# Two projections as separate runs with a stored partial sum, in a single-core hybrid layer

## The chip, the cores and the metric

The kernel runs on one core of a Trainium2 chip. A core has a matrix engine (TensorE, PE in the profile; its weight loads are the row PEld), a vector engine (DVE), a scalar engine (ACT), a general engine (POOL) and a queue engine (SP) that issues most transfers. PE writes to PSUM, eight banks of 128 x 512 floats; DVE and ACT read them from there. The metric is the device time of one execution in microseconds, the median of several runs.

## The reference, cut to what matters

One layer works on 2048 latent tokens of width 1024. One input projection feeds two token mixers, branch A (a gated DeltaNet, four heads of 128) and branch B (windowed attention, eight heads of 64). Each branch is gated, projected to width 1024 by a matrix of its own, scaled by a sigmoid gate computed from the input, and the two are summed:

```
def _merge(ya, yb, ga, gb, w_proj_a, w_proj_b, w_out):
    y = jax.nn.sigmoid(ga) * (ya @ w_proj_a) + jax.nn.sigmoid(gb) * (yb @ w_proj_b)
    return y @ w_out
...
    x = x + gate[:, None] * _merge(ya, yb, ga, gb, w_proj_a, w_proj_b, w_out)
```

The change concerns the two products with w_proj_a and w_proj_b, their scaling and their sum.

## The kernel before, in words

All values are float32. A product is made of three matmuls on rounded parts: each operand is split into a high part and a low part, and high x high, high x low and low x high are summed in one PSUM bank. The 2048 tokens are worked on in four groups of 512 (0 to 3).

The order is: modulation and normalisation; the input projections with the short convolutions; the triangular inverses of branch A beside the gate projections of groups 2 and 3; the scan of branch A beside gates of groups 1 and 0; attention; the branch projections (`project`); the output product (with seven products for each pair of 256-token units instead of eight). Intermediate tensors go to DRAM and come back: `yasp` and `ybsp` hold the two gated branches, `gasp` and `gbsp` the gates (as tanh values), `ysp` the merged result, one tensor for each group.

A planner orders each engine's instructions ahead of time. Work traced earlier has the higher priority, and later work fills in where the planner's own clock sees an engine free. Engines then run their lists in order. Only the output stage has its order on DVE, ACT, POOL and PE written out by hand.

Attention takes query blocks of 128 tokens in the order of groups 1, 2, 0, 3, and each block in two units (one for each key-value head), 32 units in all. A unit's scores are computed two units ahead. While attention runs it holds seven PSUM banks, and everything else on PE shares one bank (tag `acc`). Two kinds of other work fill PE there. First come the gate tiles that the scan has left over: `gates` (L841) runs column tiles 15 to 23, each for group 1 and then for group 0, 24 matmuls a tile. Then comes `project` (L1234) for groups 1, 2 and 0. Group 3 needs attention's last units and runs behind it, with all eight banks.

`project` makes eight tiles of 128 output columns for a group. A tile has two halves of 12 matmuls (L1247 to L1249), the first with branch A and w_proj_a, the second with branch B and w_proj_b, and each half has a bank of its own. DVE scales each half by its gate (L1258: gate plus one, times PSUM), with the gate loaded into tile `ta` or `tb`; POOL (DVE for group 3) adds them (L1263), and the sum is stored into `ysp`. `ta` uses two buffers with the tag `rt`, `tb` two of a pool of its own. `paced(i)` (L877) keeps the matmuls of a half behind the last matmul of attention's unit i: tiles of group 1 behind units 7 to 14, of group 2 behind 15 to 22, of group 0 behind 23 to 30.

`load_y` (L1216) loads the two branches of a group in pieces of 256 KB through the two staging buffers tagged `wr`, and splits them (ACT rounds, L1227; DVE subtracts, L1228). Branch A's parts lie in buffers that the gate weights used (`wh`, `wl`), branch B's in buffers of their own. `proj_w` (L1202) loads w_proj_a and w_proj_b through the same staging buffers, in two column halves, each with both matrices. Their tiles take the place of the input of groups 0 (w_proj_a) and 1 (w_proj_b), so each waits for the last gate that reads that group.

For group 3, tiles 6 and 7 keep both halves in PSUM. `late_sum` (L1267) scales and adds them in the output stage, at places in its hand-written order on DVE, ahead of splits that its products wait for.

## Time and profile before

| what | value |
|---|---|
| time, median of 3 runs | 1997.59 us (1997.26 to 2005.6) |
| profiled execution, its own time | 1992.9 us |
| its span, first to last instruction | 1991.2 us |
| mean granted TensorE clock | 0.989 of full speed |
| PE busy | 1917.4 us, 96% of the span |
| DVE, ACT, POOL busy | 1502.1, 802.6 and 692.1 us |
| bytes moved by DMA | 333.12 MB, mean 167 GB/s |
| projections' matmuls (L1247 to L1249) | 256 of each, the first starting at 1464.7 us |

Times in the trace are counted from the first instruction. A row of the timeline reads: start, duration, engine, line, operation, what it writes and reads, its shape, and in brackets how long the engine had stood idle before it and what ended that. A matmul's end is modelled, and the next one starts before it, so durations of PE overlap. A row whose engine has a q behind its name is an issue by that engine's sequencer, most often of a transfer.

### The profile page before, as it was taken

Reading aid. Unit: us, or ns where it says so; the run is one execution under the profiler, and the core shown is the slowest. Engines: PE = TensorE matmul, PEld = TensorE weight load, DVE = VectorE, ACT = ScalarE, POOL = GpSimd, SP = SyncE. Lnnn points to the kernel's source line nnn. Section 1 sums busy time; section 2 is a strip of 40 time slices with the busy share of each in tenths; the row PEclk is TensorE's granted clock in tenths of the full one; section 3 lists DMA queues with packets and bytes.
Section 4 is the critical chain, followed back from the end, with each engine's and each line's share of the span. In section 5 each row is a group of like instructions: output and inputs, shape, how many; then the busy total and the mean of one; then the engine's idle time right before and its main releaser. Section 6 shows DMA issues by size and latency. Waiting matters only on the chain. (4 is left out here: it accounts for less than half of the span.)

```text
span 1991.2 us, 32088 instructions
## 1 busy us (share of the span) xinstructions
PE 1917.4 (96%) x10947; PEld 1605.6 (81%) x10947; DVE 1502.1 (75%) x2869; ACT 802.6 (40%) x1994; POOL 692.1 (35%) x768
## 2 busy tenths in 40 slices
PE   7999999989999999999999999999989999999998
PEld 4888888779998787877888888788778887877786
DVE  6979766668776999999677776536686878747888
ACT  5755545554443323111222233225665656532221
POOL 2742211235542202004222234323555443420675
PEclk9999999999999999999999999999999999999999
DMA  7552226765547633528977877674455655455454
GB/s 263 173 142 87 91 89 161 195 157 175 151 134 196 170 106 116 145 89 237 230 232 225 240 212 207 178 216 146 143 176 171 185 161 164 119 173 190 141 169 135
DMA packets 387703, 333.12 MB, mean 167 GB/s; under 512 B 83992, under 2 KB 307536, under 8 KB 386900
## 3 DMA queue, kind: packets, MB, share of 16 engines
q1 hardware_dynamic: 352244, 288.60, 50.1%
q10 hardware_dynamic: 35296, 42.48, 6.1%
q8 instruction: 87, 1.43, 0.3%
q14 instruction: 76, 0.62, 0.1%
HBM read 220.28 MB, written 109.13 MB: 165 GB/s over the span
## 5 line engine op out<-in xcount | busy, mean ns | idle before, releaser
L535 PE MATMUL rps<-hh,wh 128*128 128x512 f32 x768 | 309.3, 403 | 3.7 <-DVE rt L829 2.5
L537 PE MATMUL rps<-hh,wl 128*128 128x512 f32 x768 | 307.6, 401 | 0.0
L536 PE MATMUL rps<-hl,wh 128*128 128x512 f32 x768 | 307.5, 400 | 0.0
L574 DVE SCALAR_TENSOR_TENSOR cacc<-y,cw,cacc 128x512 f32<-128x512 f32 (+1 forms) x224 | 164.0, 752 | 22.2 <-ACT cacc L572 18.3
L535 PEld LDWEIGHTS rps<-hh,wh 128*128 128x128 f32 x768 | 145.3, 189 | 39.4 <-DVE rt L829 3.3
L535 PE MATMUL lps<-hh,wh 128*128 128x512 f32 (+1 forms) x448 | 171.8, 384 | 0.3 <-ACT y L645 0.3
L536 PE MATMUL lps<-hl,wh 128*128 128x512 f32 (+1 forms) x448 | 171.5, 383 | 0.0
L537 PEld LDWEIGHTS rps<-hh,wl 128*128 128x128 f32 x768 | 145.2, 189 | 32.6
L536 PEld LDWEIGHTS rps<-hl,wh 128*128 128x128 f32 x768 | 145.5, 189 | 31.9
L537 PE MATMUL lps<-hh,wl 128*128 128x512 f32 (+1 forms) x448 | 171.0, 382 | 0.0
L961 DVE TENSOR_TENSOR pl<-pt,ph 128x512 fp32r<-128x512 f32 x156 | 105.4, 685 | 42.9 <-ACT ph L959 42.1
L959 ACT CAST ph<-pt 128x512 fp32r<-128x512 f32 x156 | 90.2, 585 | 110.2 <-PE pt L957 77.0
L827 ACT ACTIVATE rt<-rps 128x512 f32<-128x512 f32 x96 | 57.3, 597 | 185.0 <-PE rps L537 169.0
L933 DVE CUSTOM_DVE_ANT_0 pr<-sc,band,sk 128x640 f32<-128x640 f32 (+1 forms) x128 | 106.6, 862 | 32.1 <-PE sc L929 16.2
L943 POOL TENSOR_SCALAR pr<-pr,sm 128x640 f32<-128x640 f32 (+1 forms) x128 | 99.7, 802 | 56.5 <-DVE sm L941 39.3
L760 DVE TENSOR_TENSOR N<-N,btmp 128x62 f32<-128x62 f32 (+30 forms) x124 | 116.7, 941 | 3.0
L758 DVE TENSOR_TENSOR btmp<-N 128x62 f32<-128x62 f32 (+30 forms) x124 | 116.4, 939 | 3.1
L935 ACT ACTIVATE pr<-pr,sm 128x640 f32<-128x640 f32 (+1 forms) x128 | 104.0, 815 | 20.5 <-DVE sm L933 20.4
L246 DVE TENSOR_TENSOR wl<-wr,wh 128x512 fp32r<-128x512 f32 x120 | 92.4, 783 | 24.4 <-POOL wh L245 22.1
L1247 PE MATMUL pps<-yh,wph 128*128 128x512 f32 x256 | 105.6, 414 | 4.7 <-DVE tb L1258 2.5
L245 POOL TENSOR_SCALAR wh<-wr 128x512 fp32r<-128x512 f32 x72 | 48.8, 692 | 169.8 <-PE lps L536 97.1
L1248 PE MATMUL pps<-yl,wph 128*128 128x512 f32 x256 | 101.8, 399 | 0.0
(378 smaller groups left out, 5025.4 us busy)
## 6 DMA issues: line engine op xcount, KB each, us to landing
wr<-in_w_in_dram SPq DMA_DIRECT2D x120, 256.0 KB
kw<-Ksp SPq DMA_DIRECT2D x28, 384.0 KB
x<-vsp SPq DMA_DIRECT2D x36, 256.0 KB
k<-ksp SPq DMA_DIRECT2D x34, 256.0 KB
kT<-kTsp SPq DMA_DIRECT2D x34, 256.0 KB
wm<-in_w_mod_dram SPq DMA_DIRECT2D x16, 512.0 KB
xt<-in_x_dram SPq DMA_DIRECT2D x16, 512.0 KB
dtl<-Dsp SPq DMA_DIRECT2D x32, 256.0 KB
```

The lines of the kernel that those rows point to most:

```text
L535: T.matmul(ps, lhsT=wh[:, k], rhs=xh[:, k], start=k == 0, stop=False)
L536: T.matmul(ps, lhsT=wh[:, k], rhs=xl[:, k], start=False, stop=False)
L537: T.matmul(ps, lhsT=wl[:, k], rhs=xh[:, k], start=False, stop=k == kt - 1)
L574: V.scalar_tensor_tensor(a, y[:, t:t + n], cw[:, m, t:t + 1], a, op0=ALU.mult, op1=ALU.add)
L758: V.tensor_tensor(tv, A[:, m + 1:, m].unsqueeze(2).to_broadcast([h1 + n, r, m]), A[:, m, 0:m].unsqueeze(1).to_broadcast([h1 + n, r, m]), o ...
L760: V.tensor_tensor(A[:, m + 1:, 0:m], A[:, m + 1:, 0:m], tv, op=ALU.add)
L933: V.tensor_tensor_reduce(s_, ps[:, o:768], band[:, b0:b0 + W + 256], -0.125, sk[:, 1, hd:hd + 1], ALU.add, ALU.min, sm[:, h, 1:2])
L935: S.activation(s_, s_, AF.Exp, scale=-1.0, bias=sm[:, h, 1:2], accum_out=sm[:, h, 2:3])
L943: G.tensor_scalar(p[:, h, :W + 256], p[:, h, :W + 256], sm[:, h, 3:4], 1.0, op0=ALU.mult, op1=ALU.mult)
L961: V.tensor_tensor(pl, pt, f32(ph), op=ALU.subtract)
L1247: T.matmul(ps, lhsT=wh[:, k, ms], rhs=hs[k], start=k == 0, stop=False)
L1248: T.matmul(ps, lhsT=wh[:, k, ms], rhs=ls[k], start=False, stop=False)
```

## The change

The two halves of a tile no longer run side by side. `first_half` makes branch A's product, scales it by its gate and stores it in DRAM, in a new tensor `ypsp`. `second_half` makes branch B's product, loads the stored partial sum into `ta` and the gate into `tb`, scales, adds and stores the sum into `ysp`.

First halves of group 1 stand behind attention's units 3 to 6, two behind each unit. Second halves of groups 1, 2 and 0 stand behind units 7 to 30, one behind each, where the tiles with both halves stood. Among them come the first halves of groups 2 and 0, two for three units, behind units 7 to 17 and 19 to 29. Group 3 runs after attention: eight first halves, six second halves, and two second halves left in PSUM for `late_sum`, which now loads the stored partial sum too.

`load_y` loads one branch at a time, A into the pool's buffers and B into those of the gate weights (the other way round than before). `proj_w` loads w_proj_a whole, then w_proj_b, and gives way after each column half. The last two gate tiles, 22 and 23, run by group: both for group 0, then both for group 1 (`last_gates`).

```
+    ypsp = many("ypsp", 4, [128, KT, 512])
...
+    def last_gates(ms):
+        jobs = [rest(ev, m, False) for m in ms]
+        for gi in (0, 1):
+            for m, job in zip(ms, jobs):
+                rest_run(ev, job, m, gi)
...
-        for j in range(2):
-            cs_ = slice(j * 512, j * 512 + 512)
-            for a, nm in enumerate(("w_proj_a", "w_proj_b")):
-                wh, wl = wp[a]
+        for a, nm in enumerate(("w_proj_a", "w_proj_b")):
+            wh, wl = wp[a]
+            for j in range(2):
+                cs_ = slice(j * 512, j * 512 + 512)
...
-            yield
+                yield
...
-        for src, po, tags in ((yasp, wq, ("wh", "wl")), (ybsp, pool, ("ybh", "ybl"))):
+    def load_y(pool, gi, a):
+        src, po, tags = ((yasp, pool, ("yah", "yal")), (ybsp, wq, ("wh", "wl")))[a]
...
-    def project(pool, wp, gi, yy=None, first=-99, late=()):
+    def half(yy, a, m, i):
+        ps = acc([128, 512], name="pps")
+        ms = slice(m * 128, m * 128 + 128)
+        (wh, wl), (hs, ls) = wp[a], yy
+        with paced(i):
+            for k in range(4):
+                T.matmul(ps, lhsT=wh[:, k, ms], rhs=hs[k], start=k == 0, stop=False)
+                T.matmul(ps, lhsT=wh[:, k, ms], rhs=ls[k], start=False, stop=False)
+                T.matmul(ps, lhsT=wl[:, k, ms], rhs=hs[k], start=False, stop=k == 3)
+        return ps
+
+    def first_half(yy, gi, m, i=-1):
+        ps = half(yy, 0, m, i)
+        t = ev.tile([128, 512], F32, name="ta", tag="rt", bufs=2)
+        dma(t, gasp[gi][m])
+        V.scalar_tensor_tensor(t, t, 1.0, ps, op0=ALU.add, op1=ALU.mult)
+        dma(ypsp[gi][:, m], t)
+
+    def second_half(pool, yy, gi, m, i=-1):
+        ps = half(yy, 1, m, i)
+        ta = ev.tile([128, 512], F32, name="ta", tag="rt", bufs=2)
+        dma(ta, ypsp[gi][:, m])
+        tb = pool.tile([128, 512], F32, name="tb")
+        dma(tb, gbsp[gi][m])
+        V.scalar_tensor_tensor(tb, tb, 1.0, ps, op0=ALU.add, op1=ALU.mult)
+        (V if gi == 3 else G).tensor_tensor(ta, ta, tb, op=ALU.add)
+        dma(ysp[gi][:, m], ta)
+
+    def late_sum(gi, m, ps):
+        ta, tb = (pool.tile([128, 512], F32, name=nm, tag=tag, bufs=2)
+                  for pool, nm, tag in ((ev, "ta", "rt"), (wq, "tb", "wr")))
+        dma(ta, ypsp[gi][:, m])
+        dma(tb, gbsp[gi][m])
+        yield
+        V.scalar_tensor_tensor(tb, tb, 1.0, ps, op0=ALU.add, op1=ALU.mult)
+        V.tensor_tensor(ta, ta, tb, op=ALU.add)
+        dma(ysp[gi][:, m], ta)
+        yield
...
-    gates(list(range(BESIDE, 24)), (1, 0))
+    gates(list(range(BESIDE, 22)), (1, 0))
+    last_gates((22, 23))
...
         next(halves)
-        yy = load_y(pj, 1)
+        ya = load_y(pj, 1, 0)
+        next(halves)
+        for m in range(KT):
+            first_half(ya, 1, m, 3 + m // 2)
+        next(halves)
+        yb = load_y(pj, 1, 1)
         next(halves)
         for j, gi in enumerate((1, 2, 0)):
-            project(pj, wp, gi, yy, 8 * j + 8 + PACE)
-            yy = None
+            for m in range(KT):
+                i = 8 * j + 8 + m + PACE
+                second_half(pj, yb, gi, m, i)
+                for f in range(16):
+                    if 7 + 3 * f // 2 == i:
+                        g_ = (2, 0)[f // 8]
+                        if f % 8 == 0:
+                            ya = load_y(pj, g_, 0)
+                        first_half(ya, g_, f % 8, i)
+            if j < 2:
+                yb = load_y(pj, (2, 0)[j], 1)
...
-        sums67 = project(pj, wp, 3, late=(6, 7))
+        ya = load_y(pj, 3, 0)
+        for m in range(KT):
+            first_half(ya, 3, m)
+        yb = load_y(pj, 3, 1)
+        for m in range(6):
+            second_half(pj, yb, 3, m)
+        sums67 = [late_sum(3, m, half(yb, 1, m, -1)) for m in (6, 7)]
```

More of the change, by code (lines that the diff above doesn't have):

```diff
@@ L1234, in project @@
-    def project(pool, wp, gi, yy=None, first=-99, late=()):
-        yy = yy or load_y(pool, gi)
-        left = []
-        for m in range(KT):
-            i = first + m
-            us = []
-            ms = slice(m * 128, m * 128 + 128)
-            for j, tsp in enumerate((gasp, gbsp)):
-                ps = acc([128, 512], name="pps")
-                (wh, wl), (hs, ls) = wp[j], yy[j]
-                with paced(i):
-                    for k in range(4):
-                        T.matmul(ps, lhsT=wh[:, k, ms], rhs=hs[k], start=k == 0, stop=False)
-                        T.matmul(ps, lhsT=wh[:, k, ms], rhs=ls[k], start=False, stop=False)
-                        T.matmul(ps, lhsT=wl[:, k, ms], rhs=hs[k], start=False, stop=k == 3)
-                if m in late:
-                    us.append((ps, tsp))
-                    continue
-                if j == 0:
-                    t = ev.tile([128, 512], F32, name="ta", tag="rt", bufs=2)
-                else:
-                    t = pool.tile([128, 512], F32, name="tb")
-                dma(t, tsp[gi][m])
-                V.scalar_tensor_tensor(t, t, 1.0, ps, op0=ALU.add, op1=ALU.mult)
-                us.append(t)
-            if m in late:
-                left.append(late_sum(gi, m, us))
-                continue
-            (V if gi == 3 else G).tensor_tensor(us[0], us[0], us[1], op=ALU.add)
-            dma(ysp[gi][:, m], us[0])
-        return left
```

38 lines of the change are left out of this document (11 added, 27 removed).

## The prediction

> **What bounds the kernel now.** I read the page first. TensorE (PE) is busy for nearly the whole span; no other engine comes near it.
>
> ```profile
> span 1991.2 us, 32088 instructions
> PE 1917.4 (96%) x10947; PEld 1605.6 (81%) x10947; DVE 1502.1 (75%) x2869; ACT 802.6 (40%) x1994; POOL 692.1 (35%) x768
> ```
>
> The change adds and removes no matmul, so it can only win time in which PE isn't fed. A busy PE is a modelled thing here (a 0.39 us matmul overlaps the next one), so I count starts, not busy time. The timeline of PE in the last gates shows twelve matmuls of 512 columns from one start to the other, 2.80 us, so 0.233 us each; I write 0.234.
>
> ```profile
> 1414.73 0.40 PE L535 MATMUL rps<-hh,wh 128*128 128x512 f32 x1
> ...
> 1417.53 0.39 PE L535 MATMUL rps<-hh,wh 128*128 128x512 f32 x1
> ...
> 1420.42 0.48 PE L537 MATMUL rps<-hh,wl 128*128 128x512 f32 x1
> ```
>
> The last of these rows is the last gate matmul, at 1420.4. Next come windows cut at the ends of attention's units (a unit is a query block and a key-value head; its end is its last L964). The columns are the window, its length, then busy us and instructions of PE, weight load, DVE, ACT and POOL, then granted clock, DMA share and GB/s. The second fence has the same windows for instructions on the projections' PSUM tile alone.
>
> ```profile
> 1423.10:1464.50 41.40, 34.40 (x187) 25.99 (x186) 33.93 (x77) 33.07 (x73) 28.00 (x28) 1.00 0.61 193
> 1464.50:1478.40 13.90, 12.30 (x71) 10.40 (x70) 11.43 (x27) 9.17 (x21) 4.88 (x5) 1.00 0.20 60
> 1521.00:1558.40 37.40, 37.40 (x212) 31.72 (x211) 27.53 (x61) 20.26 (x46) 16.75 (x18) 1.00 0.42 126
> 1464.50:1768.20 303.70, 295.21 (x1605) 247.84 (x1603) 224.46 (x469) 169.38 (x365) 138.72 (x143) 0.99 0.51 156
> ```
>
> ```profile
> 1423.10:1464.50 41.40, 0.00 (x0) 0.00 (x0) 0.00 (x0) 1.00 0.61 193
> 1464.50:1478.40 13.90, 5.96 (x22) 4.00 (x22) 0.67 (x1) 1.00 0.20 60
> 1521.00:1558.40 37.40, 18.29 (x72) 13.10 (x72) 4.09 (x6) 1.00 0.42 126
> 1464.50:1768.20 303.70, 148.01 (x576) 105.18 (x576) 32.03 (x47) 0.99 0.51 156
> ```
>
> Between 1521.0 and 1558.4 three whole units ran with 72 projection matmuls between them and PE never idle: (37.4 - 72 x 0.234) / 3 = 6.85 us is what attention needs of PE per unit. Units 4 to 7 lie between 1423.1 and 1464.5 with no projection matmul and no gate left: 41.4 / 4 = 10.35 us each, set by the round trip PE, ACT, DVE, PE. So 41.4 - 4 x 6.85 = **14.0 us of PE are empty there**. From 1464.5 to 1768.2 the same sum gives 303.7 - 24 x 6.85 - 576 x 0.234 = 4.5 us, a little more in truth as two blocks have fewer keys.
>
> **The change part by part.**
>
> *First halves of group 1 behind units 3 to 6.* Eight halves of 12 matmuls, 96 x 0.234 = 22.5 us, go into the empty stretch. It grows to at least 27.4 + 22.5 = 49.9 us (8.5 longer), and 22.5 us leave what follows: -14.0 us at best, 0 if nothing arrives in time. What has to arrive is w_proj_a and the first branch's tile. Now each waits for the last gate, and this is SP's queue of issues:
>
> ```profile
> 1423.76 0.35 SPq L1211 DMA_DIRECT2D wpr<-in_w_proj_a_dram  x1
> ...
> 1442.77 0.33 SPq L1211 DMA_DIRECT2D wpr<-in_w_proj_b_dram  x1
> ```
>
> Eight weight pieces in 19 us are 2.5 us a piece through the two "wr" buffers. The reordered last gates end group 0 48 matmuls early (11.2 us of PE, with attention's share between them some 20 us), and w_proj_a's tiles take group 0's place, so four pieces and the four of the branch (8 x 2.5 = 20 us) are there about when unit 3 ends, at 1423. I take 2 us lost: **-12**, between -14 and 0.
>
> *Unit 8 loses its cover.* Now its first filler is a first half, ready at once; the second half waits for the second branch, finished only by unit 7.
>
> ```profile
> 1464.72 0.48 PE L1247 MATMUL pps<-yh,wph 128*128 128x512 f32 x1
> ...
> 1474.93 0.50 PE L1247 MATMUL pps<-yh,wph 128*128 128x512 f32 x1 [1.60 <-ACT yh L1227]
> ```
>
> 10.2 us lie between them. After the change the halves at this place are second halves; the next first halves (group 2) need a load that stands in the two "wr" buffers behind the second branch's four pieces and four of w_proj_b. Unit 8 then runs bare, 10.35 - 6.85 = 3.5 us empty against 13.9 - 6.85 - 22 x 0.234 = 1.9 now: +1.6, and unit 9 gets one half instead of two. I take **+2**, from 0 (other loads overtake) to 3.5.
>
> *Thinner filler in units 8 to 31.* 24 second halves and 16 first halves, 480 matmuls instead of 576, in the pattern two, two, one half per unit. A unit with one half is 6.85 + 12 x 0.234 = 9.66 us of PE, under the bare 10.35: 0.7 us empty, eight times, 5.5 at most; nothing where late halves slide in. I take **+2**.
>
> *The extra round trip.* 32 stores and 32 loads of 256 KB. DVE and POOL do as many operations as before. On SP it is 64 issues of 0.33 to 0.43 us, hidden while SP is idle; behind a store that waits for DVE or for the matmul stand attention's key and query loads. DMA moves 16 MB more over some 340 us, 50 GB/s on 156; the page's stretches go to 250 and more, so this is hidden in attention. The dear part is the buffer: both kinds of half now use the two "ta" buffers, 16 times a group instead of 8. Per unit that is at most two uses in some 11 us, which two buffers bear. The last group has no attention to stretch it, and there it counts.
>
> *The start of the last group.* The gap at attention's end, and what follows it:
>
> ```profile
> 1767.80 0.40 PE L964 MATMUL av<-pl,vc 128*128 128x512 f32 x1
> 1770.67 0.50 PE L1247 MATMUL pps<-yh,wph 128*128 128x512 f32 x1 [2.48 <-DVE tb L1258]
> ...
> 1771.76 0.63 PE L1248 MATMUL pps<-yl,wph 128*128 128x512 f32 x1
> ...
> 1774.74 0.55 PE L1249 MATMUL pps<-yh,wpl 128*128 128x512 f32 x1
> ```
>
> PE stood for 2.5 us, and then eight matmuls went from 1771.76 to 1774.74, 0.43 us apart instead of 0.23: 1.6 us more. The first branch's buffers now come free with the half behind unit 29, not with the last projection of group 0, so its load is done before attention ends and there is something to run. Between -4 and 0; **-3**.
>
> *The last group itself.* Now its 16 halves end at 1816.88, two products of w_out follow, and the third pair starts late. The chain on the other side is the "ta" buffer:
>
> ```profile
> 1789.42 2.29 DVE L1353 TENSOR_TENSOR B11l<-B,B11h 128x2048 fp32r<-128x2048 f32 x1 [7.11 <-ACT B11h L1380]
> 1794.74 0.32 SPq L1264 DMA_DIRECT2D ysp<-ta  x1
> 1799.64 1.60 SPq L1257 DMA_DIRECT2D ta<-gasp  x2
> 1803.67 0.69 DVE L1258 SCALAR_TENSOR_TENSOR ta<-ta,pps 128x512 f32<-128x512 f32 x1 [0.64 <-DMA ta<-gasp]
> 1804.98 0.32 SPq L1264 DMA_DIRECT2D ysp<-ta  x1
> 1807.08 2.22 SPq L1257 DMA_DIRECT2D ta<-gasp  x2
> 1817.38 0.99 SPq L1272 DMA_DIRECT2D ta<-gasp  x2
> 1821.86 0.69 DVE L1275 SCALAR_TENSOR_TENSOR ta<-ta,pps 128x512 f32<-128x512 f32 x1 [4.61 <-DMA ta<-gasp]
> 1823.80 0.69 DVE L1367 TENSOR_TENSOR al<-yA,ah 128x512 fp32r<-128x512 f32 x1
> ```
>
> ```profile
> 1816.88 0.39 PE L1249 MATMUL pps<-yh,wpl 128*128 128x512 f32 x1
> ...
> 1827.88 0.39 PE L1483 MATMUL P<-B21h,al 128*128 128x512 f32 x1
> 1829.45 0.50 PE L1481 MATMUL P<-B22h,ah 128*128 128x512 f32 x1 [1.18 <-ACT ah L1363]
> ```
>
> A load into "ta" takes 4.0 us until its use (1799.64 to 1803.67), its store holds the buffer for 2.1 (1804.98 to 1807.08) to 4.9 us (1794.74 to 1799.64). The scaling is 0.69 us. A first half thus holds a buffer for 6.8 to 9.6 us under this traffic, and perhaps 5.4 with a load of 2.6 where the queues are emptier: per half, with two buffers, 2.7 to 4.8 us against PE's 2.8. I take 3.4, as it mostly falls before w_out's transfers: 27 us for eight. Second halves add 0.7 us for the sum; the stores of now stand some 10 us apart per pair with two scalings each, I take 8 us a pair, 24 for three pairs. With 3 us until the first half is done and 4.5 for the late load (1817.38 to 1821.86), the late sum stands at 58 us after the group's start; now it is 1821.86 - 1770.67 = 51. The fourth product's left operand is split 1.9 us after it (1823.80), at 60. PE needs it after 45 us of halves and three products of 2.8, at 53. So PE will wait about 7 us where it now loses about 1 to 3: **+6**, between 0 (2.7 per half) and +22 (4.8, and DVE's wait for w_out of 7.1 us ahead of the scalings).
>
> The Trainium skill, page "DMA: Bandwidth & Descriptors", section "Anatomy of one DMA — SWDGE (gpsimd) path", speaks against a round trip of this kind: a fixed cost of about 2.0 us, mostly the receipt of the write, longest into HBM, plus bytes over 436 GB/s. By it (an estimate, as the section is on another issuing path) a 256 KB transfer is 2.6 us, a first half holds its buffer 5.9 us, and the sum of the last group would be about 0 instead of +6; the stores' 2.1 and 4.9 us here lie on both sides of it.
>
> **Sum.** -12 + 2 + 2 - 3 + 6 = -5 us. The profiled execution took 1992.9 us (1991.2 of span and 1.7 around it), so 1987.9 there; it is 4.7 us under the median of the runs shown, 1997.59, and I carry the difference over: 1992.6, said as **1992**.
>
> **The rivals.**
>
> *The last group isn't held up.* If "ta" is emptied as fast as PE fills it, the +6 is 0 and units 8 to 31 lose 2 together: -12 + 2 - 4 = -14, **1984**. For it: the first branch's scalings start before attention's end, when DMA is light, and the late sum has one scaling less. Against it: the rows above, where stores hold the buffer up to 4.9 us.
>
> *The filler comes late.* The first halves need weights and branch through the same two buffers; if these come only when the gates have ended as now, eight pieces from 1423.8 put the first half at 1444, two units late. Then half of the 14 us is left, -7, and the same costs stand: -7 + 2 + 2 - 3 + 6 = 0, **1998**. For it: 2.5 us a piece. Against it: the last gates' order frees group 0's place.
>
> *Slower: the "ta" buffers hold up w_out.* DVE works in order. If its wait for w_out's first block (7.1 us above) stands ahead of the first branch's scalings, no buffer turns over meanwhile; at 4.8 us per half the late sum comes at 58 + 11 + 7 = 76 us, and the last group costs the 22 of its upper bound: -11 + 22 = +11, **2009**. It decides from about 4.0 us per half, where 8 x 0.6 = 5 us come on the 6 and eat the 11 won before. For it: DVE did wait there; against it: first halves begin some 20 us ahead of w_out's block.
>
> **How the numbers follow.** I give the forecast 0.42, the last group not held up 0.29, late filler 0.16, slower 0.13. 0.5% is 10 us, about what a measurement of this kernel can tell from no change, so faster is below 1987.6 and slower above 2007.6. Faster: 0.29 and a fifth of the forecast's 0.42, 0.37. Slower: most of the last rival, 0.12, and 0.02 of late filler, where both come together: 0.14. Same: the rest, 0.49. The forecast's own range is 1985 to 2000; with the others **1978 to 2008**.
>
> **What would show it.** Right: no stretch like units 4 to 7 without L1247's successors; units 4 to 7 at about 12.5 us each; unit 8 bare; PE running a projection across attention's end; at the fourth product a wait of PE for the split behind the late sum. Wrong: first halves beginning later than unit 4, a last group whose late sum stands under 53 us from its start, or attention's ACT and DVE work stretched past 12.5 us a unit by the denser filler.

## The result, and the profile after

The kernel with the change takes 2016.3 us (median of 6 runs, 2013.35 to 2022.34); beside it the kernel before took 1997.42. The ratio is 1.0103 [1.0070, 1.0135]: slower by more than the prediction's 0.5%, and above the upper end of the forecast's range, 2008. The page of the profile after starts:

```profile
span 2013.9 us, 32227 instructions
...
PE 1923.7 (96%) x10947; PEld 1605.6 (80%) x10947; DVE 1505.2 (75%) x2869; ACT 802.5 (40%) x1994; POOL 689.2 (34%) x768
...
DMA packets 396920, 349.91 MB, mean 174 GB/s; under 512 B 85016, under 2 KB 308560, under 8 KB 396116
```

Same matmuls, 16.8 MB more traffic, 22.7 us more span in these two profiled executions (the medians differ by 18.9). To see where, I cut the windows of PE at the ends of attention's units again: units 4 to 7, units 8 to 11, and units 4 to 31, first for all instructions, then for the projections' PSUM tile alone.

```profile
1428.40:1485.70 57.30, 53.84 (x283) 44.53 (x282) 38.27 (x80) 33.23 (x71) 26.62 (x27) 0.98 0.62 194
1485.70:1528.50 42.80, 37.73 (x208) 29.23 (x207) 36.58 (x79) 32.46 (x70) 24.40 (x25) 1.00 0.61 185
1428.40:1775.40 347.00, 332.20 (x1790) 274.38 (x1789) 260.01 (x541) 200.19 (x430) 160.07 (x167) 0.99 0.62 191
```

```profile
1428.40:1485.70 57.30, 25.00 (x96) 17.99 (x96) 5.43 (x8) 0.98 0.62 194
1485.70:1528.50 42.80, 6.62 (x21) 3.58 (x21) 0.68 (x1) 1.00 0.61 185
1428.40:1775.40 347.00, 149.66 (x577) 105.46 (x578) 32.76 (x48) 0.99 0.62 191
```

The first halves are where they were meant to be: 96 matmuls in units 4 to 7. But the four units took 57.3 us instead of 49.9, and units 8 to 11, which had 96 projection matmuls before, have 21.

A ledger makes kernels with different filler comparable. *Net* is the time of a point less 0.234 us for each projection matmul begun by then, counted from the last gate matmul (1420.4 before, 1421.3 after), because the stretch up to there, the same in all kernels but for the order of the last gate tiles, ended between 1414 and 1429 us in the profiles. The last group is the time from its last projection matmul to the last product of w_out.

| | before | after | difference |
|---|---|---|---|
| net at the end of unit 3 | 2.7 | 7.1 | +4.4 |
| units 4 to 7 | 41.4 | 34.9 | -6.5 |
| units 8 to 11 | 34.0 | 37.9 | +3.9 |
| units 12 to 31 | 134.9 | 139.2 | +4.3 |
| attention's end to the last projection, net | 3.8 | 4.5 | +0.7 |
| last projection to last product | 166.1 | 181.2 | +15.1 |

The sum, 21.9, and 0.9 at the last gate are the 22.7. So attention lost 6.1 us instead of winning 8, and the last group lost 15.1 instead of 6.

The first row of the ledger is a stop of PE in the middle of unit 3. ACT's timeline shows what it waited for, PE's that it followed, and SP's the issue:

```profile
1419.31 0.62 ACT L1233 CAST yh<-yr 128x512 fp32r<-128x512 f32 x1 [4.29 <-DMA yr<-yasp]
1421.26 0.62 ACT L1233 CAST yh<-yr 128x512 fp32r<-128x512 f32 x1 [1.33 <-DMA yr<-yasp]
1423.29 0.62 ACT L1233 CAST yh<-yr 128x512 fp32r<-128x512 f32 x1 [1.41 <-DMA yr<-yasp]
1423.81 0.58 ACT L966 CAST ph<-pt 128x512 fp32r<-128x512 f32 x1
```

```profile
1421.33 0.40 PE L538 MATMUL rps<-hh,wl 128*128 128x512 f32 x1
1424.44 0.80 PE L970 MATMUL av<-ph,vc 128*128 128x512 f32 x1 [2.72 <-ACT ph L966]
```

```profile
1411.26 0.41 SPq L1232 DMA_DIRECT2D yr<-yasp  x1
...
1414.58 6.42 SPq L1232 DMA_DIRECT2D yr<-yasp  x2
```

A piece issued at 1411.26 could be rounded at 1419.31. ACT works in order: attention's own cast (L966) stood behind three rounds of pieces that hadn't landed.

In the last group DVE's timeline has the wait that the forecast's last rival named, and PE waits at the fourth product, where the forecast said it would (the first row is w_out's first product, the third the start of the fourth):

```profile
1799.88 2.29 DVE L1374 TENSOR_TENSOR B11l<-B,B11h 128x2048 fp32r<-128x2048 f32 x1 [10.84 <-ACT B11h L1401]
...
1846.48 0.69 DVE L1277 TENSOR_TENSOR ta<-ta,tb 128x512 f32<-128x512 f32 x1 [1.26 <-DMA yA<-ysp]
```

```profile
1824.86 0.39 PE L1502 MATMUL P<-B11h,ah 128*128 128x512 f32 x1
...
1835.27 0.80 PE L1503 MATMUL P<-B21l,ah 128*128 128x512 f32 x1 [4.47 <-DVE B21l L1374]
1845.79 0.80 PE L1502 MATMUL P<-B21h,ah 128*128 128x512 f32 x1 [5.29 <-ACT ah L1384]
...
1847.82 0.80 PE L1504 MATMUL P<-B21h,al 128*128 128x512 f32 x1 [0.81 <-DVE al L1388]
```

The late sum stands 21.6 us behind w_out's first product (4.7 before), the fourth product 20.9 (8.3 before). But the 5.29 us aren't a wait for the late sum. ACT's own row shows what they wait for, the load of the fourth product's left operand (a piece of group 1's sum, stored long before):

```profile
1839.85 0.40 ACTq L1369 DMA_DIRECT2D yA<-ysp  x1
...
1845.12 0.62 ACT L1384 CAST ah<-yA 128x512 fp32r<-128x512 f32 x1 [34.42 <-DMA yA<-ysp]
```

ACT issued it 15.0 us behind w_out's first product; before, it was 0.2. In the trace the issue waits for a semaphore (a counter that tells of a transfer's landing) on which a store of a second half, issued by SP at 1837.64, landed at 1839.78. The forecast's chain, late sum and then DVE's split, ends right behind it and costs PE the last 0.81 us.

### The profile page after: what moved, and what is told of

Its sections match the earlier page's. It is cut to its first block, busy times and chain, and to the rows that moved or that the text cites. A ratio compares the mean times of both kernels' runs of the same rounds, so it can differ in the third digit from the quotient of the medians.

```text
span 2013.9 us, 32227 instructions
## 1 busy us (share of the span) xinstructions
PE 1923.7 (96%) x10947; PEld 1605.6 (80%) x10947; DVE 1505.2 (75%) x2869; ACT 802.5 (40%) x1994; POOL 689.2 (34%) x768
## 5 line engine op out<-in xcount | busy, mean ns | idle before, releaser
L966 ACT CAST ph<-pt 128x512 fp32r<-128x512 f32 x156 | 90.0, 584 | 98.3 <-PE pt L964 64.5
L942 ACT ACTIVATE pr<-pr,sm 128x640 f32<-128x640 f32 (+1 forms) x128 | 104.1, 815 | 22.8 <-DVE sm L940 22.7
```

Of the source, the lines that this page charges most:

```text
L942: S.activation(s_, s_, AF.Exp, scale=-1.0, bias=sm[:, h, 1:2], accum_out=sm[:, h, 2:3])
```

## The experiments

Each was timed in three rounds beside the kernel before. The ratios are of times, the ledger is of one profiled execution each:

| kernel | ratio to before | net: unit 3 | unit 7 | unit 11 | unit 31 | last projection to last product |
|---|---|---|---|---|---|---|
| before | 1 | 2.7 | 44.1 | 78.1 | 213.0 | 166.1 |
| after | 1.0103 | 7.1 | 42.0 | 79.9 | 219.1 | 181.2 |
| after, last group as before | 1.0067 [1.0046, 1.0088] | 4.2 | 40.0 | 79.6 | 217.8 | 171.4 |
| before, last group as after | 1.0093 [1.0064, 1.0122] | 2.7 | 43.9 | 75.6 | 211.4 | 188.5 |
| after, later first halves of groups 2, 0 | 1.0102 [1.0064, 1.0140] | 5.5 | 41.6 | 75.9 | 219.3 | 183.5 |
| the same, w_proj_b earlier, last group as before | 1.0094 [1.0064, 1.0125] | 6.9 | 43.9 | 77.0 | 225.1 | 170.7 |
| after, rounding on POOL | 1.0055 [1.0040, 1.0070] | 2.3 | 31.0 | 70.8 | 208.0 | 181.1 |
| **before, rounding on POOL** | **0.9958 [0.9943, 0.9973]** | 2.7 | 41.1 | 70.9 | 203.0 | 165.9 |
| before, round trip's traffic alone | 1.0052 [1.0036, 1.0068] | 2.7 | 43.2 | 78.3 | 218.3 | 168.6 |
| before, rounding on POOL, traffic | 1.0010 [0.9995, 1.0025] | 2.7 | 43.2 | 73.6 | 218.3 | 169.5 |
| group 1 alone moved | 1.0065 [1.0042, 1.0088] | 6.3 | 41.6 | 79.6 | 215.4 | 174.5 |
| group 1 alone, rounding on POOL | 0.9997 [0.9982, 1.0012] | 2.4 | 31.1 | 68.3 | 202.6 | 174.3 |
| the same, second halves a unit later | 0.9988 [0.9973, 1.0004] | 2.4 | 31.1 | 70.9 | 203.1 | 173.1 |
| all of it moved, POOL, last group as before | 0.9989 [0.9973, 1.0006] | 2.4 | 31.1 | 68.7 | 201.3 | 167.9 |
| after, w_out's split behind the scalings | 1.0141 [1.0124, 1.0158] | 4.1 | 40.1 | 79.3 | 218.8 | 188.8 |
| after, five "ta" buffers in the last group | 1.0161 [1.0137, 1.0185] | 5.3 | 42.0 | 80.8 | 223.3 | 192.7 |
| after, last group's gate loads left out | 1.0106 [1.0078, 1.0135] | 7.1 | 41.5 | 80.1 | 218.8 | 178.0 |
| both of these two cuts | 1.0113 [1.0082, 1.0144] | 6.9 | 41.7 | 80.4 | 219.7 | 176.2 |

Kernels with the same code in attention (after and the five that change its last group) give 217.8 to 223.3 at unit 31, five of the six within 217.8 to 219.7: differences of 2 us in a column say nothing.

### Which half of the change costs

First the two halves of the change apart. Theory A had most of the loss in the last group's chain of scalings, rival B in the 16 MB, which slow every load. The last group as before (both halves of a tile side by side, nothing stored between them), in the kernel after:

```
-        for m in range(KT):
-            first_half(ya, 3, m)
...
+        sums67 = project3(pj)
```

> The changed kernel, but the last group (group 3) as in the kernel before: both halves of a tile side by side, no stored partial sum, two late sums of two scalings each. Theory A (of the 19 us lost, about 15 are lost behind attention's end, in the last group's chain of `ta` buffers, DVE and w_out): 2016 - 15 = 2001, PE between the last projection and the end as long as in the kernel before. Rival B (the 16 MB of extra traffic slow all loads, and the last group has a quarter of them): 2016 - 5 = 2011.

The last group as after, in the kernel before:

> The kernel before, but the last group alone as in the changed kernel: eight first halves stored, then second halves. Theory A: 1997 + 15 = 2012. Rival B: 1997 + 5 = 2002. If the two parts add up, this run's loss and the gain of the run before it are the same number.

The new last group put on the kernel before costs 188.5 - 166.1 = 22.4 us in the ledger and 17.9 in the time (2009.12 against 1991.20), which is theory A's side. Taking it out of the kernel after wins 9.8 in the ledger, but only some 7 us by the ratios, nearer to rival B's number than to A's. The parts don't add up: with the old last group on the changed attention, 171.4 - 166.1 = 5.3 us stay lost. The timeline of ACT in the kernel with group 1 alone moved, which has the old last group too (174.5), against the kernel before shows one cause, in the load of the fourth product's left operand. Each fence has ACT's issue, its split, and SP's issue of the output gate, first with group 1 moved, then before:

```profile
1819.82 0.43 ACTq L1393 DMA_DIRECT2D yA<-ysp  x1
...
1831.87 0.62 ACT L1408 CAST ah<-yA 128x512 fp32r<-128x512 f32 x1 [16.60 <-DMA yA<-ysp]
...
1818.17 0.43 SPq L1538 DMA_DIRECT2D gbc<-gsp  x1
```

```profile
1817.36 0.42 ACTq L1348 DMA_DIRECT2D yA<-ysp  x1
...
1823.14 0.62 ACT L1363 CAST ah<-yA 128x512 fp32r<-128x512 f32 x1 [8.23 <-DMA yA<-ysp]
...
1818.42 0.42 SPq L1493 DMA_DIRECT2D gbc<-gsp  x1
```

The 256 KB could be split 12.0 us after their issue instead of 5.8. Before, they were issued 1.1 us ahead of `gbc` (512 KB) and the four `xr` blocks of 256 KB that follow it; here 1.7 us behind `gbc`. The window in which PE stands has the queues full (DMA share 1.09, 342 GB/s):

```profile
1825.00:1830.00 5.00, 0.92 (x5) 0.42 (x3) 0.00 (x0) 0.00 (x0) 0.00 (x0) 0.99 1.09 342
```

That those loads hold it up is read from the order of the issues; no run moved them. It was issued late for the reason seen in the kernel after: its semaphore was that of SP's gate load for the late sum, which landed at 1819.72. With the new last group the issue stands 6.5 to 19.1 us behind w_out's first product, and in all these runs but the one with five buffers it follows such a landing within 0.1 us. This load is a possible cause of the last group's loss that no run tested by itself.

Then theory A's reason for attention: that group 2's first half holds the one bank in units 8 to 11. Its edit is `if 10 + 5 * f // 4 == i` in place of `if 7 + 3 * f // 2 == i`; the second kernel also loads w_proj_b's second half ahead of the second branch and has the old last group.

> The changed kernel, with the first halves of groups 2 and 0 behind units 10 to 28 (10 + 5f/4) instead of 7 to 29 (7 + 3f/2), so that the second halves behind units 7 to 10 stand ahead of them on PE. Theory A for the stage (units 8 to 11 ran bare, 10.5 us empty, because a first half of group 2 held the one PSUM bank while its branch was still loading, with second halves ready behind it): 8 to 10 us less, 2007. Rival B (loads are slow for all of them): no change, 2016.

> Both together: the last group as before, the first halves of groups 2 and 0 later, and the second half of w_proj_b loaded ahead of the second branch instead of behind it. Theory A: 2016 - 15 - 10 = 1991, faster than the kernel before by some 6 us. Rival B: 2016 - 5 = 2011.

Both times came nearer to rival B's numbers than to A's. Units 8 to 11 did win 3 to 4 us net (75.9 and 77.0 against 79.9), with 60 projection matmuls instead of 21, but all of it was lost again by unit 31. The order of the halves matters in those units, but it isn't the cause of the loss.

### Waits in order

From unit 2 to attention's end ACT's rows add up to 14.6 us of waits for weight pieces and 21.6 for branch pieces. The next experiment takes the rounding off the engines on which attention's own loop stands:

```
-                    S.copy(wh[:, k, cs_], wr)
+                    G.tensor_scalar(wh[:, k, cs_], wr, 1.0, 1.0, op0=ALU.mult, op1=ALU.mult)
...
-            last["yh", k] = S.copy(yh[:, k % 2], yr)
-            last["yl", k] = V.tensor_tensor(yl[:, k % 2], yr, f32(yh[:, k % 2]), op=ALU.subtract)
+            if gi == 3:
+                last["yh", k] = S.copy(yh[:, k % 2], yr)
+            else:
+                G.tensor_scalar(yh[:, k % 2], yr, 1.0, 1.0, op0=ALU.mult, op1=ALU.mult)
+            last["yl", k] = (V if gi == 3 else G).tensor_tensor(yl[:, k % 2], yr, f32(yh[:, k % 2]), op=ALU.subtract)
```

> The kernel after the change, with the rounding of the weight and branch pieces taken off ACT, and the branches' low part off DVE, both onto POOL (group 3 as it was; 2.0 us a piece on POOL instead of 0.62 and 0.68 us). Theory C, waits in order: ACT waits 14.6 us for weight pieces and 22.9 us for branch pieces from unit 2 to attention's end, with attention's own casts behind it, and each of the now seven loads in attention brings a gap of PE (2.9 us at 1421, 2.7 at 1481, 1.8 at 1501, 1.4 at 1511, 1.8 at 1597, 2.5 at 1633, 1.9 at 1686). Then these gaps go, unit 3 ends near 1423 as before instead of 1428.4, attention ends at 1765 to 1768 instead of 1775.4, and the ratio to before is about 1.006. Rival D, too little ready filler: the pieces come no earlier, POOL's own waits delay the scaling of the scores, and attention ends within 2 us of 1775 or later; ratio 1.010 or more.

The same in the kernel before:

> The kernel before the change, with the same moves of the pieces' rounding and low part to POOL. Theory C: the gaps of PE at branch and weight pieces that the kernel before has too (1.9 us at 1472.8, 2.3 at 1502.2, 2.5 at 1569 to 1572, 1.9 at 1671 to 1673) go, 6 to 8 us, attention ends near 1761 instead of 1768.2, ratio about 0.9965. Rival D: these gaps come back as halves that start later, as each piece takes 0.7 us longer to prepare and stands on POOL behind other work; attention ends at 1768 or later, ratio 1.000 to 1.003.

Theory C held in both, close to its numbers. The first window is units 4 to 7 of the kernel after with this edit, the second those of the kernel before with it:

```profile
1417.70:1468.90 51.20, 51.20 (x283) 43.26 (x282) 37.42 (x82) 27.92 (x61) 34.45 (x38) 1.00 0.66 204
```

```profile
1418.50:1456.90 38.40, 32.14 (x187) 25.81 (x185) 35.95 (x74) 27.26 (x61) 32.64 (x37) 1.00 0.59 188
```

Now 96 projection matmuls cost 51.2 - 38.4 = 12.8 us instead of their 22.5, PE is never idle there, and unit 3 ends as before. The kernel before with this edit is the fastest of all, 1983.21 us beside 1989.61.

But the edit wins as much in the kernel before as in the kernel after, so the change costs the same with it: 1.0055 / 0.9958 = 1.0097 in the ratios, against 1.0103, and 208.0 - 203.0 = 5.0 us at unit 31, against 6.1. ACT's waits are what ate the first step in units 3 to 7; they are not why the change is slower at the end.

### What the round trip's traffic costs

The kernel before, with its gate loaded twice and its scaled half stored once more, and nothing reordered:

```
+                if j == 0 and gi != 3:
+                    dma(t, tsp[gi][m])
                 dma(t, tsp[gi][m])
                 V.scalar_tensor_tensor(t, t, 1.0, ps, op0=ALU.add, op1=ALU.mult)
+                if j == 0 and gi != 3:
+                    dma(ypsp[gi][:, m], t)
```

> The kernel before the change, with the round trip's traffic alone: for groups 1, 2 and 0 each first half's gate is loaded twice into its "ta" buffer and its scaled half is stored once more, so 24 loads and 24 stores of 256 KB, 12.6 MB; no order of the work is changed. Rival B, the traffic slows the loads that attention and the halves wait for: attention ends 4 us or more later than 1768.2, ratio 1.002 to 1.004. Theories A and C: PE's stops come from the order of the waits, not from the bytes; attention's end moves by under 2 us and the ratio is 0.999 to 1.001.

And with the rounding on POOL:

> The kernel before with the pieces' rounding on POOL, and with the same 24 loads and 24 stores more in groups 1, 2 and 0 that cost 0.5% where ACT rounds the pieces. If the traffic costs time only through ACT's and DVE's waits for pieces in order, it is free here: ratio 0.995 to 0.997, attention's end within 2 us of the run without it, counted from the last gate. If the bytes or the "ta" buffers cost by themselves, 4 us or more come back: ratio 0.998 to 1.002.

Rival B is right about the first: 12.6 MB cost 218.3 - 213.0 = 5.3 us by attention's end, and 10.1 in the time (1999.68 against 1989.61). ACT shows a part of it; pieces land later, here group 0's first (with the traffic, then before):

```profile
1675.19 1.32 ACT L1228 CAST yh<-yr 128x512 fp32r<-128x512 f32 x2 [4.14 <-DMA yr<-yasp]
```

```profile
1670.27 1.26 ACT L1227 CAST yh<-yr 128x512 fp32r<-128x512 f32 x2 [2.48 <-DMA yr<-yasp]
```

That the traffic would be free with the rounding on POOL was wrong. The ledger has 218.3 - 203.0 = 15.3 us, from the slowest of ten executions; the ratios, 1.0010 against 0.9958, say some 10 us, the same as with the rounding on ACT. So ACT's and DVE's waits for pieces don't make the price. One stop of PE shows another reason: the gate's second load stands behind its first in the same buffer, it could be used only 8.5 us after its issue (1523.75), DVE waits for it in order, and PE for DVE:

```profile
1532.28 0.69 DVE L1264 SCALAR_TENSOR_TENSOR ta<-ta,pps 128x512 f32<-128x512 f32 x1 [5.97 <-DMA ta<-gasp]
```

```profile
1533.03 0.79 PE L1251 MATMUL pps<-yh,wph 128*128 128x512 f32 x1 [5.48 <-DVE ta L1264]
...
1537.88 0.63 PE L1253 MATMUL pps<-yh,wpl 128*128 128x512 f32 x1
```

Two loads in a row into one buffer hold it longer than the change's own halves do, so I take this as more than the change's own round trip costs.

### Group 1 alone

The change's first step without the splitting of groups 2, 0 and 3, whose tiles have both halves side by side as before; rounding on POOL, then on ACT:

```
+        for m in range(KT):
+            second_half(pj, yb, 1, m, 8 + m + PACE)
+        for j, gi in ((1, 2), (2, 0)):
+            project(pj, gi, 8 * j + 8 + PACE)
```

> The change's first step alone, with the pieces' rounding on POOL: group 1's first halves behind units 3 to 6 with the stored partial sum, its second halves behind 7 to 14, one a unit; groups 2, 0 and 3 with both halves side by side as before. With the pieces on POOL and nothing moved, units 4 to 7 took 38.4 us without a projection matmul, 38.4 - 4 x 6.85 = 11.0 us of PE empty. Theory (the forecast's first step holds where nothing waits for pieces in order and groups 2 and 0 aren't split): units 4 to 7 take 50 to 52 us with 96 projection matmuls, units 8 to 14 with 12 matmuls each take 9.7 to 10 us, and 8 to 10 us of the 11 are kept at attention's end: ratio 0.990 to 0.992. Rival (the filler taken out of units 8 to 14 is missed there, as a unit with 12 matmuls has idle time of its own): ratio 0.995 or more.

> The same as the run with group 1's first halves moved alone, but with the pieces' rounding on ACT and DVE as in both kernels. Theory C (waits in order eat the step): the gap at unit 3 and those at the second branch's pieces remain, about 5 and 4 us of the 14 empty ones, traffic is 4 MB instead of 17, and the ratio is 0.996 to 1.000. Rival (the splitting of groups 2 and 0 and their traffic are the whole of the loss): ratio 0.992 to 0.995.

With the rounding on POOL the rival was right: units 4 to 7 won the 10 us (31.1 net at unit 7 against 41.1) and at unit 31 nothing is left (202.6 against 203.0); the last group, with the late operand load above, then adds 8.4. With it on ACT both theories missed: the ratio is no better than for the whole change with the old last group, 1.0067, so splitting groups 2 and 0 isn't the whole of the loss. It isn't free either: at unit 31 the kernels with the split stand 2.4 us higher with the rounding on ACT (217.8 against 215.4), about the spread of that column, and 5.4 on POOL (208.0 against 202.6). The timeline of PE and of POOL at the start of unit 8:

```profile
1479.19 0.49 PE L1249 MATMUL pps<-yh,wph 128*128 128x512 f32 x1 [2.76 <-POOL yh L1236]
1480.54 0.80 PE L1250 MATMUL pps<-yl,wph 128*128 128x512 f32 x1 [0.85 <-POOL yl L1237]
```

```profile
1478.52 0.62 POOL L1236 TENSOR_SCALAR yh<-yr 128x512 fp32r<-128x512 f32 x1 [6.52 <-DMA yr<-ybsp]
```

PE waits for the second branch (not for w_proj_b, as my next expectation had it): its rows are attention's own output, complete only with units 6 and 7, and a second half can't begin before they are stored, loaded and rounded. The next kernel starts the second halves one unit later (`9 + m + PACE`), and the last one of this kind does the whole change so, with w_proj_b ahead of the second branch, first halves of groups 2 and 0 behind units 11 to 29 and the last group as before.

> The run with group 1's first halves moved alone and the pieces' rounding on POOL, with the second halves of group 1 one unit later (behind units 8 to 15). In that run 10 us were won in units 4 to 7, unit 8 then lost 8 us (PE stood 2.9 and 1.1 us for w_proj_b's pieces in its second half, and the clock was low behind it), and seven units with 12 projection matmuls lost some 0.6 us each. Theory: the 8 us go, attention's end comes about 198 us of net time behind the last gate (end less 0.234 us for each projection matmul) instead of 202.6, and the ratio is 0.992 to 0.996, at least level with the kernel before with the rounding on POOL (0.9958). Rival: a later second half is missed in units 8 to 9 in the same amount, ratio 0.998 or more.

> The whole change in attention with what the runs showed against it taken out: rounding of the pieces on POOL, w_proj_b whole before the second branch, second halves one unit later, first halves of groups 2 and 0 behind units 11 to 29, five in six units' places, and the last group as before the change. Theory (the round trip costs through the "ta" buffers and the waits in order only): units 4 to 7 at 51 us with 96 projection matmuls, no stop in unit 8, ratio 0.993 to 0.998. Rival (12.6 MB and 32 turns more of the two "ta" buffers cost wherever they are put, as the traffic alone cost 0.5% with the rounding on ACT and on POOL): ratio 1.000 or more, so that the best kernel keeps both halves of groups 2 and 0 side by side.

The first of these theories failed, the second stands between its two numbers. The stop got no shorter: unit 8 is bare, unit 9 waits 3.0 us for the same piece (with group 1 alone moved), and at unit 11 the net is 70.9, exactly that of the kernel that moved nothing.

```profile
1485.30 0.51 PE L1249 MATMUL pps<-yh,wph 128*128 128x512 f32 x1 [3.01 <-POOL yh L1236]
```

So the first step moves PE's empty time from units 4 to 7 into 8 to 11; it doesn't fill it. The whole change in this order has the ratio 0.9989, group 1 alone 0.9988 in the same rounds, and the nets at unit 31 lie 1.8 us apart. So the split of groups 2 and 0 (8.4 MB more and the extra turns of "ta") costs nothing here that the times can tell, where it cost 5.4 us in the kernel after's places. That speaks for places rather than bytes, but it isn't shown apart from the earlier w_proj_b; and this best order of the change still stands 0.3% behind the kernel before with the rounding on POOL.

### The last group

Three cuts at the two suspected causes, DVE's wait for w_out's first block and the turn of the two buffers. The split behind all first-half scalings:

```
-            with tc.issue_after(last["yh", 3].ins), tc.issue_after(last["yl", 3].ins):
+            with tc.issue_after(last["yh", 3].ins), tc.issue_after(last["fh"].ins):
                 S.copy(hi["B11"], B["B11"])
```

> The kernel after the change, with one order changed: on DVE and ACT the split of w_out's first block comes behind all eight first-half scalings of group 3 (it stood behind three of them). Theory A, wait in order: DVE's 10.84 us wait for that block holds both "ta" buffers while five scalings are ready, so without it the late sum (1846.5 us, 21.6 us behind w_out's first product) comes 7 to 10 us earlier, the fourth product starts some 12 to 14 us behind the first one instead of 20.9, and the time is about 8 us under the kernel after (ratio to before about 1.006). Rival, the buffers' round trip itself: two buffers at 5 to 7 us a use set the pace whatever DVE's order is; the eighth scaling still ends near 1820, the late sum moves by under 3 us, w_out's first split comes later, and the time is the kernel after's or up to 5 us more (ratio 1.010 to 1.013).

The rival was right: without DVE's wait the scalings are no faster, each waiting for its gate.

```profile
1778.45 0.68 DVE L1256 SCALAR_TENSOR_TENSOR ta<-ta,pps 128x512 f32<-128x512 f32 x1
...
1792.90 0.69 DVE L1256 SCALAR_TENSOR_TENSOR ta<-ta,pps 128x512 f32<-128x512 f32 x1 [7.49 <-DMA ta<-gasp]
...
1801.22 0.69 DVE L1256 SCALAR_TENSOR_TENSOR ta<-ta,pps 128x512 f32<-128x512 f32 x1 [3.05 <-DMA ta<-gasp]
1804.86 0.69 DVE L1256 SCALAR_TENSOR_TENSOR ta<-ta,pps 128x512 f32<-128x512 f32 x1 [2.95 <-DMA ta<-gasp]
...
1814.34 0.69 DVE L1256 SCALAR_TENSOR_TENSOR ta<-ta,pps 128x512 f32<-128x512 f32 x1 [3.39 <-DMA ta<-gasp]
```

From the first to the eighth it is 35.9 us, 5.1 each; in the kernel after 38.3. The late sum came 2.9 us later behind attention's end, and the time was no better (1.0141). Next, more buffers, three of them in the place of attention's score tiles (`ar.tile([128, 4, 640], F32, name="ta", tag="pr", bufs=3)`):

> The kernel after the change, with five buffers instead of two for the last group's "ta" tiles (three of them take the place of attention's score tiles, free by then). Theory, the two buffers set the last group's pace (5.1 us per first half where DVE's wait for w_out's block is out of the way, 35.9 us from the first scaling to the eighth, against PE's 2.8 us a half): the scalings then follow PE, the eighth ends 22 to 26 us after the first, the late sum stands at most 12 us behind w_out's first product instead of 21.6, and the ratio to before falls from 1.010 to 1.014 to 1.003 to 1.006. Rival, the transfers themselves are slow while w_out's blocks are loaded: the gates' loads take as long with five buffers, the eighth scaling stands 32 us or more behind the first, and the ratio stays at 1.009 or more.

This one tells little. The eighth scaling stood 18.2 us behind the first, but w_out's blocks lie where those buffers are, so their loads began only at 1817.85 and PE stood 16.1 us before the first product. Buffers and w_out's transfers were both out of the way at once. So the load was cut instead (`if gi != 3: dma(t, gasp[gi][m])`, the scaling reading a tile in SBUF), alone and together with the order above:

> The kernel after the change, with the last group's eight first halves scaled by a tile that lies in SBUF already instead of their gates (another result: the first branch's gate of that group is left out); the eight gate loads of 256 KB into "ta" go, the stored partial sums and the two buffers stay. Theory, the buffers' turn (load, scaling, store: 5.1 us a first half under w_out's transfers) sets the last group's pace: without the load a turn is the store and the scaling, so the eighth first-half scaling stands about 20 us behind the first instead of 36 to 38, the late sum comes 8 us or more earlier, and the ratio to before is 1.003 to 1.008. Rival, it is w_out's own blocks and DVE's wait for the first of them: the late sum moves by under 4 us and the ratio stays at 1.010 or more.

> The kernel after the change with both single cuts in the last group together: the eight gate loads of its first halves left out (scaled by a tile in SBUF instead, so the first branch's gate of that group is missing from the result), and DVE's and ACT's split of w_out's first block behind all eight first-half scalings. Each alone moved the late sum little: with the order alone the eighth scaling stood 35.9 us behind the first, with the loads alone 35.2 us. Theory, two limits of the same length side by side (the "ta" buffers' turn, and DVE's wait of 9 to 11 us for w_out's first block): with both out the eighth scaling stands 20 to 24 us behind the first, the late sum comes at most 60 us behind attention's end (71.1 in the kernel after, 74.0 and 68.5 with one cut), and the ratio is 1.002 to 1.006. Rival, neither sets it, but the second halves' two loads each behind w_out's transfers: the late sum stays at 66 us or more behind attention's end, ratio 1.009 or more.

In the times neither shows a gain: the ratios, 1.0106 and 1.0113 against 1.0103, are the rivals'. In the ledger the loads alone won 3.2 us, and the rival held there too: DVE's wait of 9.0 us for w_out's block was then what held the scalings.

```profile
1795.15 2.29 DVE L1375 TENSOR_TENSOR B11l<-B,B11h 128x2048 fp32r<-128x2048 f32 x1 [9.02 <-ACT B11h L1402]
```

Together the two cuts won 5.0 in the ledger, and the late sum came 62.7 us behind attention's end instead of 71.1, between the two expectations. What is left is a third wait, for a buffer's store, in the stretch where w_out's four blocks of 1 MB are under way:

```profile
1790.78 1.28 DVE L1257 SCALAR_TENSOR_TENSOR ta<-yh,pps 128x512 f32<-128x512 f32 x2
1803.29 0.69 DVE L1257 SCALAR_TENSOR_TENSOR ta<-yh,pps 128x512 f32<-128x512 f32 x1 [11.23 <-DMA ypsp<-ta]
```

```profile
1797.50 15.59 SPq L1258 DMA_DIRECT2D ypsp<-ta  x7
```

The last scaling before the wait ended at 1792.06. So 5.4 of the 11.2 us passed before SP issued the first of the stores (it had to wait for a semaphore on which a load of `yA`, issued by ACT, landed at 1797.44), and 5.8 from the issue to DVE's next scaling.

So several waits of about the same length stand side by side, and each cut uncovers the next. Of the 15.1 us the ledger puts 5.0 down to these two, which the times don't confirm; how the rest divides between the stores, the second halves' loads and the operand load that ACT issues late stays open.

## Why the prediction was wrong, step by step

Between the forecast's -5 us and the +22.7 of the profiles lie 27.7: 14.1 in attention (-8 forecast, +6.1 measured), 3.7 at the start of the last group, 9.1 in the last group, and 0.9 ahead of all this.

**First halves of group 1, -12 us.** This step failed, on both its supports. "They are there about when unit 3 ends" held for the data, but I never asked what stands behind a piece that is a little late. On ACT it is attention's own cast: +4.4 us at unit 3, 57.3 us instead of 49.9 in units 4 to 7, so -2.1 by unit 7. (The price of 2.5 us a piece was misread: between its two rows lie six of the eight issues, so 3.8 us each. The pieces came about in time because the new order of the last gates freed the place by 1402: ACT's eight casts ran from 1402.4 to 1423.3.) And where ACT's wait is cut the gain is 10.0 at unit 7, close to the forecast, and is gone by unit 31 (202.6 against 203.0): the rows of units 8 and 9 show the second halves that follow not ready. The stretch 4 to 7 was empty for a reason that also holds for 8 and 9: half of group 1's work waits for attention's own output.

**Unit 8 loses its cover, +2 (0 to 3.5).** Right in kind, wrong in extent: not one unit but four, +3.9 as built and 10 where the casts aren't in the way (units 8 to 11 net 39.8 with group 1 moved and its second halves a unit later, 29.8 with nothing moved, both with the rounding on POOL).

**Thinner filler, +2.** +4.3 in units 12 to 31, near the 5.5 I had as its upper end. But the traffic alone, with the filler of before, cost 5.1 in the same units (140.0 against 134.9), so which of the two terms was too small stays open.

**The extra round trip, 0.** "Hidden in attention" was argued from GB/s, and that is the wrong quantity: alone, in the places of the kernel before, it cost some 10 us of time, with the rounding on ACT and on POOL; put elsewhere, nothing that the times can tell.

**Start of the last group, -3.** +0.7. PE does run a projection across attention's end, the stop of 2.5 us there is gone, as forecast; another of 2.65 us, behind a scaling, came in the middle of the group.

**The last group, +6 (0 to +22).** +15.1, inside its bounds. The term was 3.4 us per first half; measured were 5.1 with DVE free, over my upper end of 4.8. The last rival, at 0.13, was the nearest: its point of decision, 4.0 us per half, was passed. Its reason, DVE's wait ahead of the scalings, isn't borne out by itself (without it the eight scalings still took 35.9 us), and the nearness of its 2009 is in part luck: its 22 us for the last group were too many, and the 11 won before it never came. The forecast's own chain, through the late sum, missed the wait that was longer, the operand's late load. Of the signs of being right, a projection across attention's end came true; unit 8 was nearly bare (6 projection matmuls), PE's wait for the split behind the late sum was 0.81 us behind a longer one, and units 4 to 7 at 12.5 us came true only with the rounding on POOL (12.8). Of the signs of being wrong one did: units 4 to 7 took 14.3 us each.

The Trainium skill's figure for a store of 256 KB (page "DMA: Bandwidth & Descriptors", section "Anatomy of one DMA — SWDGE (gpsimd) path": 2.0 us fixed and the bytes over 436 GB/s, by which, as the prediction estimated, the last group would cost about 0) is 2.6 us, again an estimate, as the section is on another issuing path. It doesn't hold under w_out's loads: the store above took 5.8 us from its issue to the next use of its buffer.

## What to carry to other kernels

Before filling an empty stretch of the bound engine, follow what comes after it: if the next work waits for the same stretch's result, the hole only moves. Work that waits for a transfer doesn't belong on the engines that feed the bound engine step by step; here moving small casts to POOL won 0.4% in the kernel before, more than any reordering did. Bandwidth that is left doesn't price traffic: ask whose buffer and whose queue it holds up. And compare an experiment with its counterpart in the kernel before: a cut that wins the same in both doesn't explain the difference between them.

## What the runs showed of the hardware that I had not expected

A stop of PE cost more than its length: after the 5.48 us stop above, twelve matmuls took 4.85 us from the first start to the last, 0.43 apart at the end, instead of 2.57; the granted clock from 1533.0 to 1538.3 was 0.50. Transfers took longer with others under way: 12.0 us from issue to split for 256 KB where it was 5.8 in the kernel before, and 5.8 us from a store's issue to the next use of its tile with w_out's blocks under way (386 GB/s), against the 2.1 to 4.9 us that the prediction read in the kernel before. And issues of one queue waited for transfers of another: ACT's load of 1839.85 for a store of SP's, SP's stores of 1797.50 for a load of ACT's, in both by a semaphore that the two shared.
